# Second-layer scores as three 64-row products per head, two heads side by side in the array, and the PSUM banks split anew

## The chip, the core and the metric

The kernel runs on one core of one Trainium2 chip. The metric is device time in microseconds for one execution. TensorE (PE in the profile) multiplies, VectorE (DVE), ScalarE (ACT) and GpSimd (POOL) do the elementwise work, and SyncE (SP) issues the DMAs. PE writes its products into PSUM, of which a tile here is one bank (128 partitions by 512 fp32 numbers), and there are eight banks.

## What is computed

A trunk of two layers over 2048 tokens plus 16 learned meta tokens, model width 1024, in fp32. The first layer runs a sliding-window attention and a convolution branch side by side. The second layer is a stick-breaking attention with 16 heads of 64 dimensions: for every query the sigmoids of the scores are combined by a running product from the diagonal back to the first key.

```python
# second layer, per block of 128 queries (16 heads, d = 64)
z = einsum('bqhd,bkhd->bhqk', q_block, k[:, :kend]) * d ** -0.5
log_beta = log_sigmoid(z)
log_1m = where(valid, log_sigmoid(-z), 0.0)          # valid: key before query, not padding
after = cumsum(log_1m, axis=3, reverse=True) - log_1m
a = where(valid, exp(log_beta + after), 0.0)
out = einsum('bhqk,bkhd->bqhd', a, v[:, :kend])
# then: out * silu(gate) @ w_out, post-norm, residual
```

The products need more precision than one pass of the array's reduced fp32 format (fp32r) gives, so a matrix is split into a high and a low part, x = hi + lo, and a product is summed from hi·hi, hi·lo and lo·hi (and, in the scores before the change, lo·lo as well).

## The kernel before

Everything is written with a tile framework. The code emits steps, `interleave` mixes two lists of steps by weight (attention of one head pair with the projection of another), and a scheduler then sets the order of the instructions on each engine, with priorities that `tc.high_priority` raises. Each engine runs its instructions in that fixed order. An instruction that waits holds up all behind it on its engine.

The first layer (`layer0`) takes four token chunks: `stage1` projects (24 matmuls per unit of 128 output columns, `mm3` at lines 138 to 140), `stage2` does the window attention and the convolution branch, then `outp` the output projection. The second layer (`layer1`) goes over eight head pairs p and two halves of the queries hf (0: query blocks 0 to 7, 1: blocks 8 to 15). `proj(p, hf)` projects k, q, v and gate, unit by unit: 24 matmuls into one bank, then an evacuation. For k and q that is an ACT copy (line 777) and a DVE subtraction (line 778), for v an ACT copy (line 786), for the gate an ACT sigmoid (804) and a DVE multiply (805).

`attn(p, hf)` does the attention of two heads h. Queries come in pairs m of two 128-blocks x, keys in chunks of up to 512 columns, from the diagonal backwards. For each chunk:

- scores (line 907): per h and x one bank z and two matmuls of 128 rows. The stationary operand is q's high (i = 0) or low (i = 1) part, stored twice over in the 64+64 rows; the moving operand is `kst` of that head, with k's high part in rows 0 to 63 and its low part in rows 64 to 127.
- ACT reads the bank twice: `om` = sigmoid(−z) (line 914) and `be` = sigmoid(z) (line 915). The bank is free when `be` has been read.
- DVE runs the product scan `S` (line 920) and multiplies (line 921).
- PE transposes `be` by 128-column blocks into `pt` (line 939), ACT copies to `aT` (line 945), and PE adds up `av` (line 953), with the two heads in the two 64-column halves of the array, in one run per chunk at raised priority.

There are 192 such chunks (24 per head pair). Operands are loaded from DRAM by SP: `kst` once per pass, the q tiles `qt` for each m, in eight DMAs (line 883).

Eight banks are shared out as pools: `pj` 2 (projections), `pz` 3 (scores, and in the first layer also transposes and every second projection unit), `pt` 2 (transposes), `pav` 1 (`av`). In the first layer `banks = cycle(BK)` alternates `stage1`'s units between `pj` and `pz`; `pw` (line 541) and `po` (line 640), and in the second layer all projections (line 764) and the output projection (line 1004), use `pj` alone.

Of the kernel before, what the change touches and what calls it, by code (L numbers as in the profile page):

```python
# [34 lines left out]
CB = 6  # L35
PB = (2, 3, 2)
BK = ("pj", "pz")
WP = 60
AVP = 400
PRE0 = 1  # L40
PRE1 = 3
# [37 lines left out]
class Trunk:  # L79
# [108 lines left out]
    def layer0(self, after=None):  # L188
# [300 lines left out]
        def cbranch(ut):  # L489
# [44 lines left out]
            def pw():  # L534
                ch, cl = S["ch"], S["cl"]
                gb = w2.tile([P, 4, 272], F32, tag="gb", name="gb", bufs=1)
                nc.sync.dma_start(gb[:, :, :N], gbd[:, :, b0 : b0 + N].rearrange("r p t -> p r t"))
                for m in range(4):
                    if m % 2 == 0:
                        wh, wl = self.weights(pww, a["w_pw2"][m // 2], w2, "yl", f"wp{m // 2}")  # L540
                    ps = self.bank("pj", "pw")
                    for k in range(4):
                        kk = 4 * (m % 2) + k
                        self.mm3(ps[:, :N], wh[:, kk], wl[:, kk], ch[:, k, :N], cl[:, k, :N], k == 0, k == 3)
                    tt = w2.tile([P, 272], F32, tag="ctt", name="mc")
                    nc.vector.tensor_tensor(tt[:, :N], ps[:, :N], gb[:, m, :N], ALU.mult)
                    nc.sync.dma_start(md[4 + m, :, b0 : b0 + N], tt[:, :N])
# [78 lines left out]
        def outp(t):  # L626
# [3 lines left out]
            def mm(nh):  # L630
# [8 lines left out]
                w = slice(nh * 512, nh * 512 + 512)  # L639
                ps = self.bank("pj", "po")  # L640
                for k in range(KB):
# [91 lines left out]
    def after0(self, pool, tags):  # L733
        self.layer1_pools()
        self.evs = (pool, tags, D, 2)
        self.H, self.gates, self.tags = {}, [], cycle(("raw", "wh", "wl", "wh", "wl"))
        steps = self.load_part(0, 0) + self.load_part(0, 1)
# [8 lines left out]
        def proj(p, hf, parts=(0, 1)):  # L746
# [11 lines left out]
            def unit(m, part, c0, n, evac):  # L758
                def go():
                    th, tl, h0 = H[hf, part]  # L760
                    if m not in W:
                        W[m] = wload(m)
                    wh, wl = W[m]
                    ps = self.bank("pj", "pj1")
                    s = slice(c0 - h0, c0 - h0 + n)
                    with self.behind():
                        for k in range(KB):
                            self.mm3(ps[:, :n], wh[:, k], wl[:, k], th[:, k, s], tl[:, k, s], k == 0, k == KB - 1)
                    evac(ps[:, :n], c0, n)

                steps.append((float(n), go))
# [47 lines left out]
    def layer1(self):  # L819
# [12 lines left out]
        def attn(p, hf):  # L832
# [5 lines left out]
            def start():  # L838
                S["k"] = ks = []
                n = NM + nt * P  # L840
                for h in range(2):
                    kst = w4.tile([P, T], F32R, tag="kst", name="kst")
                    for i in range(2):
                        self.mv(kst[i * HD : i * HD + HD, :n], kd[i][p, h * HD : h * HD + HD, :n])
                    ks.append(kst)
# [30 lines left out]
            def qload(m):  # L876
                q0 = NM + m * 2 * P
                S["q"] = qs = []
                for h in range(2):
                    for i in range(2):  # L880
                        qt = w2.tile([P, 256], F32R, tag=f"q{h}{i}", name="qt")
                        for j in range(2):
                            self.mv(qt[j * HD : j * HD + HD], qd[i][p, h * HD : h * HD + HD, q0 : q0 + 256])
                        qs.append(qt)

            def pair_steps(m):
# [5 lines left out]
                def chunk(ei):  # L892
# [6 lines left out]
                    nbs = [b1 - b0 - (1 if first else 0), b1 - b0]  # L899
                    for h in range(2):  # L900
                        for x in range(2):
                            n = nbs[x] * P + mo
                            if n == 0:
                                continue
                            z = self.bank("pz", "z")
                            for i in range(2):
                                nc.tensor.matmul(z[:, :n], S["q"][2 * h + i][:, x * P : x * P + P], S["k"][h][:, k0 : k0 + n], start=(i == 0), stop=(i == 1))  # L907
                            om = w3.tile([P, 513], F32, tag="om", name="om")
# [5 lines left out]
                            nc.scalar.activation(om[:, :n], z[:, :n], AF.Sigmoid, scale=-0.125)  # L914
                            nc.scalar.activation(be[:, :n], z[:, :n], AF.Sigmoid, scale=0.125)  # L915
                            if first:
# [74 lines left out]
        def outp(t):  # L991
            S = {}

            def mm(nh):
# [8 lines left out]
                w = slice(nh * 512, nh * 512 + 512)  # L1003
                ps = self.bank("pj", "po1")
                for k in range(KB):
# [36 lines left out]
        for _, f in self.first + proj(1, 0):  # L1042
            f()
        for p in range(2, 6):
            interleave(proj(p, 0), attn(p - 2, 0))
# [83 lines left out]
```

## Time and profile before

| | us |
|---|---|
| median of 3 runs (2906.99 to 2913.82) | 2910.22 |
| the profiled execution's own time | 2916.46 |
| its span, first to last instruction | 2914.7 |
| first and last score matmul (line 907) start at | 1077.0 and 2821.9 |
| PE busy | 2742.9 (94%) |
| DVE busy | 2214.4 (76%) |
| ACT busy | 1463.5 (50%) |
| POOL busy | 775.3 (27%) |

Busy time of PE counts a matmul from its start to its modelled end, and matmuls overlap. What a matmul costs in a stream is the distance from its start to the start of the next one. A row of the timeline merges equal instructions that follow each other (x4 is four of them) and gives the start of the first. An entry such as `128*64 128x256` is a product in 128 rows and 64 columns of the array with 256 moving columns. An fp32 matmul of the program (`av`) is two rows of the trace, an fp32r one (scores, projections) is one.

### The profile page before, as it was taken

What the parts mean: (1) busy time and instruction counts of PE and PEld (TensorE: products, weight loads), DVE (VectorE), ACT (ScalarE), POOL (GpSimd) and SP (SyncE); (2) the same over time, 40 slices, a digit from 0 to 9 for tenths busy, and PEclk for the clock granted to TensorE, in tenths of its full rate; (3) what the DMA queues carried; (4) which work ended last, traced back from release to release, by engine and by line L of the source; (5) the groups of instructions that cost most, each with busy time, mean ns of one, the idle gap of its engine ahead of it and who ended that gap; (6) DMA issues with size and microseconds to landing.
All of it is one profiled execution on the core that took longest, in us unless ns stands there. A gap on an engine that the chain in (4) does not pass through costs nothing.

```text
span 2914.7 us, 49596 instructions
## 1 busy us (share of the span) xinstructions
PE 2742.9 (94%) x16110; PEld 2191.9 (75%) x16110; DVE 2214.4 (76%) x3696; ACT 1463.5 (50%) x3568; POOL 775.3 (27%) x2679
## 2 busy tenths in 40 slices
PE   7888989989899999999999899999999999999997
PEld 6877767767688898888887677777777777766876
DVE  7997878878767753666568888878888887887864
ACT  4223434332445432555545666767666766655551
POOL 4431211000000212333335632323223322333210
PEclk9899999999999999999999999999999999999999
DMA  7877779778866665444445562423232332244322
GB/s 264 279 247 224 235 242 266 232 229 249 264 188 206 216 189 155 132 135 133 121 136 175 148 168 69 120 68 109 66 103 82 94 110 73 74 129 125 113 94 90
DMA packets 303986, 462.87 MB, mean 159 GB/s; under 512 B 46640, under 2 KB 200640, under 8 KB 300656
## 3 DMA queue, kind: packets, MB, share of 16 engines
q1 hardware_dynamic: 303728, 459.70, 52.4%
q8 instruction: 129, 2.11, 0.3%
q14 instruction: 129, 1.06, 0.1%
HBM read 312.16 MB, written 142.14 MB: 156 GB/s over the span
## 4 chain that ended last, share of the span: by engine, by line
PE 68%; DVE 10%; DMA 9%; issue 5%; ACT 3%; POOL 2%; SPq 2%; DVEq 0%; ACTq 0%; POOLq 0%
PE pj L140 10%; PE pj L138 10%; PE pj L139 10%; PE z L907 7%; PE av L953 7%; PE pt L939 6%; PE po L138 4%; PE po L140 4%; PE po L139 4%; DVE y L304 3%; DMA wl<-wk 3%; DVE S L920 2%; DMA raw<-in_w_in 1%; DVE be L921 1%; DMA md<-mc 1%
## 5 line engine op out<-in xcount | busy, mean ns | idle before, releaser
L920 DVE TENSOR_TENSOR_SCAN S<-om,be 128x401 f32<-128x401 f32 (+3 forms) x512 | 536.3, 1068 | 72.4 <-ACT om L914 51.7
L914 ACT ACTIVATE om<-z 128x384 f32<-128x384 f32 (+5 forms) x768 | 377.7, 510 | 200.0 <-PE z L907 132.9
L921 DVE TENSOR_TENSOR be<-be,S 128x385 f32<-128x385 f32 (+5 forms) x768 | 413.8, 563 | 76.2 <-POOL be L912 21.8
L138 PE MATMUL pj<-th,wh 128*128 128x512 f32 (+2 forms) x1280 | 460.5, 360 | 6.9 <-DVE ev L805 3.6
L140 PE MATMUL pj<-th,wl 128*128 128x512 f32 (+2 forms) x1280 | 452.8, 354 | 0.0
L139 PE MATMUL pj<-tl,wh 128*128 128x512 f32 (+2 forms) x1280 | 450.6, 352 | 0.0
L945 ACT COPY aT<-pt 128x512 f32<-128x512 f32 (+2 forms) x672 | 333.9, 504 | 192.6 <-PE pt L939 152.9
L907 PE MATMUL z<-kst,qt 128*128 128x384 f32 (+6 forms) x1536 | 394.9, 357 | 31.3 <-ACT be L915 29.5
L915 ACT ACTIVATE be<-z 128x384 f32<-128x384 f32 (+5 forms) x768 | 375.2, 505 | 72.4 <-PE pt L939 71.7
L304 DVE SCALAR_TENSOR_TENSOR y<-u,cw,y 128x512 f32<-128x512 f32 (+1 forms) x480 | 392.1, 822 | 8.0
L939 PE MATMUL pt<-ident,be 128*128 128x128 f32 x2176 | 361.4, 280 | 17.8 <-ACT ev L794 6.2
L138 PE MATMUL pj<-hTh,wh 128*128 128x512 f32 (+2 forms) x880 | 322.9, 368 | 30.7 <-DMA wh<-wk 18.7
L140 PE MATMUL pj<-hTh,wl 128*128 128x512 f32 (+2 forms) x880 | 321.2, 367 | 30.4 <-POOL wl L128 15.4
L939 PEld LDWEIGHTS pt<-ident,be 128*128 128x128 f32 x2176 | 251.4, 141 | 113.9 <-ACT aT L945 31.4
L139 PE MATMUL pj<-hTl,wh 128*128 128x512 f32 (+2 forms) x880 | 318.5, 362 | 0.8 <-DVE hTl L186 0.8
L907 PEld LDWEIGHTS z<-kst,qt 128*128 128x128 f32 x1536 | 247.7, 190 | 76.1 <-ACT be L915 55.6
L953 PE MATMUL av<-aT,vt 128*64 128x256 f32 (+1 forms) x2304 | 281.9, 380 | 4.4 <-DVE og L971 4.3
L911 POOL MEMSET om<- 128x1 f32 x768 | 74.6, 99 | 768.9 <-DVE S L920 753.9
L138 PEld LDWEIGHTS pj<-th,wh 128*128 128x128 f32 x1280 | 241.6, 189 | 33.7 <-DVE ev L805 4.6
L140 PEld LDWEIGHTS pj<-th,wl 128*128 128x128 f32 x1280 | 240.9, 188 | 30.2 <-DVE wl L110 0.3
L139 PEld LDWEIGHTS pj<-tl,wh 128*128 128x128 f32 x1280 | 241.4, 189 | 25.1 <-issue 0.4
L920 DVE TENSOR_TENSOR_SCAN S<-om 128x257 f32<-128x257 f32 (+4 forms) x256 | 204.6, 811 | 62.8 <-POOL om L918 49.9
(177 smaller groups left out, 4482.5 us busy)
## 6 DMA issues: line engine op xcount, KB each, us to landing
raw<-in_w_in SPq DMA_DIRECT2D x98, 512.0 KB, 3.9
wh<-wk SPq DMA_DIRECT2D x66, 512.0 KB, 5.2
wl<-wk SPq DMA_DIRECT2D x66, 512.0 KB, 6.1
qt<-qhd SPq DMA_DIRECT2D x256, 64.0 KB, 2.6
qt<-qld SPq DMA_DIRECT2D x256, 64.0 KB, 2.4
wk<-wh SPq DMA_DIRECT2D x22, 512.0 KB, 5.1
wk<-wl SPq DMA_DIRECT2D x22, 512.0 KB, 4.6
kst<-khd SPq DMA_DIRECT2D x16, 516.0 KB, 7.4
```

The source lines that it names most:

```text
L138: mm(out, sh, mh, start=first, stop=False)
L139: mm(out, sh, ml, start=False, stop=False)
L140: mm(out, sl, mh, start=False, stop=last)
L304: return lambda: nc.vector.scalar_tensor_tensor(y[:, :TC], u[:, w : w + TC], cw[:, j, w : w + 1], y[:, :TC], ALU.mult, ALU.add)
L907: nc.tensor.matmul(z[:, :n], S["q"][2 * h + i][:, x * P : x * P + P], S["k"][h][:, k0 : k0 + n], start=(i == 0), stop=(i == 1))
L914: nc.scalar.activation(om[:, :n], z[:, :n], AF.Sigmoid, scale=-0.125)
L915: nc.scalar.activation(be[:, :n], z[:, :n], AF.Sigmoid, scale=0.125)
L920: nc.vector.tensor_tensor_scan(P_[:, : n + 1][:, ::-1], om[:, : n + 1][:, ::-1], om[:, : n + 1][:, ::-1], init, ALU.mult, ALU.bypass)
L921: nc.vector.tensor_tensor(bl[:, : n + 1], bl[:, : n + 1], P_[:, : n + 1], ALU.mult)
L939: nc.tensor.transpose(pt[:, o : o + P], bes[h, x][:, mo + b * P : mo + b * P + P], self.ident)
L945: cps.append(nc.scalar.copy(aT[:, lo:hi], pt[:, lo:hi]))
L953: mi = nc.tensor.matmul(av[h * HD : h * HD + HD, qc0 + x0 : qc0 + 256], S["v"][:, b0 + b, h * HD : h * HD + HD], at, start=not S["started" ...
```

## The change

1. The scores. Per head three products of 64 rows, hi·hi, hi·lo, lo·hi, replace the two of 128 rows. Head 0 lies in rows 0 to 63, head 1 in rows 64 to 127, so that the two heads' products use different halves of the array and write to different banks. A key chunk has 12 such products instead of 8. `kst` and `qt` now hold both heads, one tile for high and one for low, so a pair m loads its queries in two DMAs instead of eight (half the bytes), and k comes in two DMAs instead of four.
2. One run per key chunk. All four z tiles are taken first, the 12 products are emitted together at priority ZP = 800, and the first of them waits for the last four `be` (`zread[-4:]`), that is, until all four banks of the chunk before have been read.
3. Banks. PB goes from (2, 3, 2) to (1, 4, 2): one bank for `pj`, four for `pz`. In the first layer `pw` and `po` now alternate between the pools as `stage1` does. In the second layer units alternate before the attention starts and after it has ended; while it runs, projections and the output projection have the one bank of `pj`.

```diff
-PB = (2, 3, 2)
+PB = (1, 4, 2)
+ZP = 800
...
@@ pw and, in the same way, outp of the first layer
-                    ps = self.bank("pj", "pw")
+                    ps = self.bank(next(banks), "pw")
...
@@ proj and, in the same way, outp of the second layer
-                    ps = self.bank("pj", "pj1")
+                    ps = self.bank(next(self.free), "pj1")
...
@@ attn: start
-                for h in range(2):
+                for i in range(2):
                     kst = w4.tile([P, T], F32R, tag="kst", name="kst")
-                    for i in range(2):
-                        self.mv(kst[i * HD : i * HD + HD, :n], kd[i][p, h * HD : h * HD + HD, :n])
+                    self.mv(kst[:, :n], kd[i][p, :, :n])
...
@@ attn: qload
-                for h in range(2):
-                    for i in range(2):
-                        qt = w2.tile([P, 256], F32R, tag=f"q{h}{i}", name="qt")
-                        for j in range(2):
-                            self.mv(qt[j * HD : j * HD + HD], qd[i][p, h * HD : h * HD + HD, q0 : q0 + 256])
-                        qs.append(qt)
+                for i in range(2):
+                    qt = w2.tile([P, 256], F32R, tag=f"q{i}", name="qt")
+                    self.mv(qt, qd[i][p, :, q0 : q0 + 256])
+                    qs.append(qt)
...
@@ attn: chunk
-                    for h in range(2):
-                        for x in range(2):
+                    zs, wait = {}, self.zread[-4:]
+                    for x in range(2):
+                        n = nbs[x] * P + mo
+                        if n == 0:
+                            continue
+                        for h in range(2):
+                            zs[h, x] = self.bank("pz", "z")
+                        with tc.high_priority(offset=ZP):
+                            for i, j in ((0, 0), (0, 1), (1, 0)):
+                                for h in range(2):
+                                    r = slice(h * HD, h * HD + HD)
+                                    mi = nc.tensor.matmul(zs[h, x][:, :n], S["q"][i][r, x * P : x * P + P], S["k"][j][r, k0 : k0 + n], start=(i + j == 0), stop=(i == 1))
+                                    if wait is not None:
+                                        self.after_all(mi, wait)
+                                        wait = None
+                    for x in range(2):
+                        for h in range(2):
                             n = nbs[x] * P + mo
                             if n == 0:
                                 continue
-                            z = self.bank("pz", "z")
-                            for i in range(2):
-                                nc.tensor.matmul(z[:, :n], S["q"][2 * h + i][:, x * P : x * P + P], S["k"][h][:, k0 : k0 + n], start=(i == 0), stop=(i == 1))
+                            z = zs[h, x]
...
-                            nc.scalar.activation(be[:, :n], z[:, :n], AF.Sigmoid, scale=0.125)
+                            self.zread.append(nc.scalar.activation(be[:, :n], z[:, :n], AF.Sigmoid, scale=0.125))
...
@@ layer1
         for _, f in self.first + proj(1, 0):
             f()
+        self.free = cycle(("pj",))
...
+        self.free = cycle(BK)
         for t in range(8, NT):
```

(`self.free` and `self.zread` are set up in `after0`, with `self.free = cycle(BK)`.) Lines after the first additions move by 1 to 14: the scores are line 910 after the change, `mm3` lines 139 to 141, `om` and `be` 926 and 927, transposes 951, `aT` copies 957, `av` 965, the evacuations 779, 780, 788, 806 and 807.

What the scheduler makes of it is seen in three places of the instruction order. First the scores of a key chunk on PE, in the second half of the queries. Before (z is a score bank, pt a transpose, ptv a transpose of v):

```order
L907 MATMUL z<-kst,qt 128x256 x2
L907 MATMUL z<-kst,qt 128x384 x2
L953 MATMUL av_24083<-aT,vt_23339 64x256 x8
L939 MATMUL pt_24359<-ident,be 128x128 x4
L907 MATMUL z<-kst,qt 128x256 x2
L939 MATMUL pt_24366<-ident,be 128x128 x4
L939 MATMUL pt_24373<-ident,be 128x128 x4
L907 MATMUL z<-kst,qt 128x384 x2
L793 MATMUL ptv_24422<-ident,ev_24419 128x128
L907 MATMUL z<-kst,qt 128x384 x4
L953 MATMUL av_24083<-aT,vt_23339 64x256 x8
```

And now one chunk's run, with buffer numbers. The four banks are z_25038 (head 0, x 0), z_25039 (head 1, x 0), z_25046 (head 0, x 1) and z_25047 (head 1, x 1); the kst and qt named are the high or the low part:

```order
L910 MATMUL z_25038<-kst_23377,qt_24620 128x400
L910 MATMUL z_25039<-kst_23377,qt_24620 128x400
L910 MATMUL z_25046<-kst_23377,qt_24620 128x400
L910 MATMUL z_25047<-kst_23377,qt_24620 128x400
L910 MATMUL z_25038<-kst_23379,qt_24620 128x400
L910 MATMUL z_25046<-kst_23379,qt_24620 128x400
L910 MATMUL z_25039<-kst_23379,qt_24620 128x400
L910 MATMUL z_25047<-kst_23379,qt_24620 128x400
L910 MATMUL z_25038<-kst_23377,qt_24622 128x400
L910 MATMUL z_25046<-kst_23377,qt_24622 128x400
L910 MATMUL z_25047<-kst_23377,qt_24622 128x400
L910 MATMUL z_25039<-kst_23377,qt_24622 128x400
```

Before, the score products stood in twos and fours between other work. Now all 12 stand together, and the scheduler has put the heads in the order 0 1 0 1, 0 0 1 1, 0 0 1 1. Of the 194 runs in the program 190 have this order of heads.

Second, what lies between that run and the next on PE, and beside it on ACT. PE now:

```order
L910 MATMUL z<-kst,qt 128x400 x12
L951 MATMUL pt_24868<-ident,be 128x128 x2
L951 MATMUL pt_24873<-ident,be 128x128 x2
L951 MATMUL pt_24972<-ident,be 128x128 x4
L965 MATMUL av_24137<-aT,vt_23381 64x256 x6
L951 MATMUL pt_24979<-ident,be 128x128 x4
L910 MATMUL z<-kst,qt 128x256 x2
```

ACT now, in the same place:

```order
L926 ACTIVATE om<-z 128x400 x3
L927 ACTIVATE be<-z 128x400
L957 COPY aT<-pt_24868 128x256
L927 ACTIVATE be<-z 128x400 x2
L957 COPY aT<-pt_24873 128x256
L926 ACTIVATE om<-z 128x400
L927 ACTIVATE be<-z 128x400
```

Before, a z product waited for its own bank alone, the third back. Now the first of the next run stands behind all eight reads of ACT and the two copies among them, with 12 transposes and 6 `av` products of PE in between.

Third, two projection units that follow each other on PE, in the first half of the queries. Before:

```order
L139 MATMUL pj1_13935<-tl1_9540,wh1_13750 128x512
L140 MATMUL pj1_13935<-th1_9539,wl1_13751 128x512
L138 MATMUL pj1_13972<-th0_9537,wh1_13968 128x272
L139 MATMUL pj1_13972<-tl0_9538,wh1_13968 128x272
L140 MATMUL pj1_13972<-th0_9537,wl1_13969 128x272
```

Now:

```order
L140 MATMUL pj1_13921<-tl1_9540,wh1_13740 128x512
L141 MATMUL pj1_13921<-th1_9539,wl1_13741 128x512
L139 MATMUL pj1_13958<-th0_9537,wh1_13954 128x272
L140 MATMUL pj1_13958<-tl0_9538,wh1_13954 128x272
L141 MATMUL pj1_13958<-th0_9537,wl1_13955 128x272
```

The rows are alike, but before the second unit went into the other bank of `pj`; now it goes into the bank that the first has just filled.

More of the change, by code (lines that the diff above doesn't have):

```diff
@@ L639, in mm @@
                 w = slice(nh * 512, nh * 512 + 512)
-                ps = self.bank("pj", "po")
+                ps = self.bank(next(banks), "po")
                 for k in range(KB):
@@ L735, in after0 @@
         self.evs = (pool, tags, D, 2)
+        self.zread, self.free = [], cycle(BK)
         self.H, self.gates, self.tags = {}, [], cycle(("raw", "wh", "wl", "wh", "wl"))
@@ L1003, in mm @@
                 w = slice(nh * 512, nh * 512 + 512)
-                ps = self.bank("pj", "po1")
+                ps = self.bank(next(self.free), "po1")
                 for k in range(KB):
```

## Prediction

> **What bounds the kernel now.** I read the stretches of the span first, then the chain of waits, then the scores by shape and in order of time. In the stretches the columns are the stretch, its length, and the busy time of PE, its weight loads, DVE, ACT and POOL; the attention of the second layer runs from 1077 us, its second half of the queries from about 1600 us.
>
> ```profile
> 1077.00:1600.00 523.00, 514.57 (x3542) 445.98 (x3542) 318.41 (x501) 245.53 (x724) 195.71 (x706) 1.00 0.48 141
> 1600.00:2650.00 1050.00, 998.82 (x5976) 741.63 (x5976) 878.17 (x1154) 692.18 (x1691) 347.48 (x1526) 0.99 0.36 103
> ...
> PE 68%; DVE 10%; DMA 9%; issue 5%; ACT 3%; POOL 2%; SPq 2%; DVEq 0%; ACTq 0%; POOLq 0%
> ```
>
> PE is busy 98% and 95% of the two stretches, DVE 61% and 84%, ACT 47% and 66%, at a granted clock of 0.99 to 1.00; the chain that ended last is PE for 68% of the span. So in the changed part the time is the length of PE's instruction stream plus the stops in it. The halved q loads are worth nothing: the only wait of the scores for a transfer is the 0.2 us of the last row below.
>
> What PE waits for, four rows of its list (total us, times, longest; the second is of the first layer):
>
> ```profile
> PE z L907 <- ACT be L915: 29.5, 52, 2.1
> PE pj L138 <- DMA wh<-wk: 18.7, 9, 5.0
> PE pj L138 <- DVE ev L805: 3.6, 5, 0.7
> PE z L907 <- DMA kst<-kld: 0.2, 1, 0.2
> ```
>
> **The scores, by shape.** Five groups hold 1472 of the 1536 products:
>
> ```profile
> L907 PE MATMUL z<-kst,qt 128*128 128x384 f32 x512 | 138.3, 364 | 10.4 <-ACT be L915 9.5 <-DVE be L921 0.3
> L907 PE MATMUL z<-kst,qt 128*128 128x400 f32 x320 | 89.2, 372 | 10.2 <-ACT be L915 10.1
> L907 PE MATMUL z<-kst,qt 128*128 128x512 f32 x256 | 84.0, 421 | 5.8 <-ACT be L915 5.2
> L907 PE MATMUL z<-kst,qt 128*128 128x256 f32 x224 | 50.6, 307 | 1.4 <-ACT be L915 1.4
> L907 PE MATMUL z<-kst,qt 128*128 128x272 f32 x160 | 34.6, 312 | 3.3 <-ACT be L915 3.3
> ```
>
> Their mean durations overlap, so I take distances of starts, from places in the timeline where nothing waits (start, duration, instruction):
>
> ```profile
> 2012.13 0.52 PE L907 MATMUL z<-kst,qt 128*128 128x384 f32 x2
> 2012.49 0.39 PE L138 MATMUL pj<-th,wh 128*128 128x512 f32 x1
> ...
> 1168.57 1.25 PE L907 MATMUL z<-kst,qt 128*128 128x400 f32 x6
> 1169.66 0.28 PE L138 MATMUL pj<-th,wh 128*128 128x256 f32 x1
> ...
> 2217.95 0.62 PE L907 MATMUL z<-kst,qt 128*128 128x512 f32 x2
> 2218.41 0.40 PE L139 MATMUL pj<-tl,wh 128*128 128x512 f32 x1
> ...
> 2026.82 0.40 PE L907 MATMUL z<-kst,qt 128*128 128x256 f32 x2
> 2027.06 0.39 PE L138 MATMUL pj<-th,wh 128*128 128x512 f32 x1
> ```
>
> That is 0.36/2 = 0.18 us for 384 columns, 1.09/6 = 0.18 for 400, 0.46/2 = 0.23 for 512 and 0.24/2 = 0.12 for 256. With 0.12 for all the narrower ones, the scores take 832 × 0.18 + 256 × 0.23 + 448 × 0.12 = 262 us of PE's stream.
>
> **Term 1, the products: −33 us.** No 64-row pair is in this trace; the nearest are `av`'s products, in two 64-column halves. The second pair of rows is full-array fp32 products, for scale:
>
> ```profile
> 1700.06 0.54 PE L907 MATMUL z<-kst,qt 128*128 128x272 f32 x3
> 1700.53 1.52 PE L953 MATMUL av<-aT,vt 128*64 128x256 f32 x12
> 1701.97 0.66 PE L939 MATMUL pt<-ident,be 128*128 128x128 f32 x4
> 1702.39 0.48 PE L138 MATMUL pj<-th,wh 128*128 128x512 f32 x1
> ...
> 2647.18 1.05 PE L969 MATMUL av<-amT,zvm 128*128 128x128 f32 x8
> 2648.06 0.60 PE L939 MATMUL pt<-ident,be 128*128 128x128 f32 x4
> ```
>
> A full-array row takes 0.88/8 = 0.11 us for 128 columns, so 0.22 for 256; twelve would take 2.64 us. `av`'s twelve take 1.44: two halves do run side by side, at 0.22 per pair (six are 1.3 us) plus some overhead. I take the same of row halves. If heads alternated, 12 products would fill 6 places where there were 8, −25% or −66 us. But the order of the heads in a run is 0 1 0 1 0 0 1 1 0 0 1 1, and PE starts its products in the order of the program: the fifth product (head 0) has the sixth (head 0) behind it and runs alone, the pairs shift by one, and the twelfth runs alone too. That is 7 places: −1/8 of 262 = −33 us. Bounds: −66 (six places) and +131 (no halves side by side, 12 places).
>
> **Term 2, dividing the array: +65 us.** The `av` run also shows what a change of division costs. Before it three 272-column scores (0.12 to 0.13 each) take 0.47 instead of 0.38: +0.09. The run takes 1.44 instead of 1.30: +0.14, of which the first pair's exposed weight load is a part. Behind it four transposes take 0.42. Without a change before them they take 0.35, and the same is seen of a row-divided product (a 16-row transpose among 128-row ones):
>
> ```profile
> 349.48 0.39 PE L140 MATMUL pj<-hTh,wl 128*128 128x512 f32 x1
> 349.80 0.60 PE L525 MATMUL pt_c<-ident,yn 16*128 16x16 f32 x3
> 350.15 0.47 PE L138 MATMUL pj<-hTh,wh 128*128 128x512 f32 x1
> ...
> 2223.23 0.60 PE L939 MATMUL pt<-ident,be 128*128 128x128 f32 x4
> 2223.58 0.98 PE L907 MATMUL z<-kst,qt 128*128 128x400 f32 x4
> ```
>
> There and back is 0.09 + 0.14 + 0.07 = 0.30 us for columns. For rows it is 0.32 − 0.23 = 0.09 going in, and the three transposes take 0.35, as long as four, 0.10 more: 0.19, the lower bound, since its one product has 16 columns and hides nothing. A score run's first pair loads 128 weight columns instead of 64, half of 0.11 more, so I take 0.34 (upper bound 0.36). In the program's order the array's division changes 446 times before and 825 times after (a score run next to an `av` run costs one change, not two): 379 more, 190 there-and-backs, 65 us (36 to 68).
>
> The Trainium skill, "TensorEngine Tiling (Array Packing)", Key Properties, says that changing the tiling mode drains TensorE while different tiles of one mode work in parallel; the trace agrees on the first (0.09 us before either kind of division), and shows the second for columns only. By its "up to 2×" for 64-row products this change would be −66 us in term 1, were it not for the order of the heads.
>
> **Term 3, one bank of `pj`: +27 us.** Evacuations (mean ns behind the comma):
>
> ```profile
> L777 ACT CAST ev<-pj 128x512 fp32r<-128x512 f32 x48 | 28.2, 587 | 71.0 <-PE pj L140 67.5 <-issue 3.4
> L778 DVE TENSOR_TENSOR ev<-pj,ev 128x512 fp32r<-128x512 f32 x48 | 33.0, 689 | 48.7 <-ACT ev L777 48.7
> L786 ACT COPY ev<-pj 128x512 f32<-128x512 f32 x24 | 14.1, 589 | 26.6 <-PE pj L140 26.6
> L804 ACT ACTIVATE ev<-pj 128x512 f32<-128x512 f32 x24 | 14.8, 615 | 17.7 <-PE pj L140 17.7
> L805 DVE TENSOR_TENSOR ev<-pj,ev 128x512 f32<-128x512 f32 x24 | 16.5, 686 | 25.2 <-ACT ev L804 25.2
> ```
>
> A unit now waits until the one before has left the bank: 1.28 us for k and q (587 + 689), 0.59 for v, 1.30 for the gate, and some 0.15 of hand-over. Between neighbouring units in the new order I counted PE's other work, at 0.11 per transpose. Behind k and q units seven gaps hold nothing (short by 1.43 each, 10 us) and five hold two transposes (1.21 each, 6 us); behind v units seven hold two (0.52 each, 4 us); the rest, gates and output units among them, are short by 7 us together. The cover for all other units is the attention of the chunk, over 2 us. The sum, 27, has no idle work to fall back on, as PE runs in order; the lower bound is 15 (if only the empty gaps and those of two transposes behind k and q count), the upper 45 (ACT found busy with a sigmoid each time, 0.5 more at 36 of these places).
>
> **Term 4, all four banks at once: +20 us.** The first product of a run now holds up PE until ACT has read four banks:
>
> ```profile
> L915 ACT ACTIVATE be<-z 128x400 f32<-128x400 f32 x160 | 81.5, 529 | 17.6 <-PE pt L939 17.5
> L914 ACT ACTIVATE om<-z 128x400 f32<-128x400 f32 x160 | 81.4, 529 | 34.0 <-PE z L907 19.7 <-DVE S L920 7.9 <-issue 3.7
> L945 ACT COPY aT<-pt 128x256 f32<-128x256 f32 x160 | 62.2, 389 | 10.5 <-PE pt L939 9.9
> ```
>
> At the place shown in the order, ACT has 8 × 0.53 + 2 × 0.39 = 5.0 us to do, and can begin two places (0.36 us) before the run's end, when the first bank is complete. PE has 12 transposes (1.3), 6 `av` (1.3) and the changes of division (0.5): 3.1 us. It stands 1.5 us or longer, and transposes, `av` and the next DVE chain stand behind it. The same count over all runs is short at 42 of 189 places, by 56 us. Against it goes the wait that was there, 29.5. I take +20 rather than +27, as stops of term 3 give ACT time; bounds 0 and +40.
>
> **Everything else: 0.** In the first layer units alternate between the pools as before and a unit of 24 products covers the evacuation of the other pool's; DVE's work is unchanged, and with PE longer its 84% falls. The output projection behind the attention alternates over more banks, where PE has no stop to lose.
>
> **Sum.** −33 + 65 + 27 + 20 = +79. The profiled execution's own time was 2916.5, 6 above the median of the runs, so 2910 + 79 = 2989; I say 2990.
>
> **Rivals.** (a) *Halves fill six places*, because each row half takes its own products without regard to the other's: term 1 is −66, the time 2957; if the narrower loads also let a pair run nearer to its column rate, another −20, 2937. For it: `av`'s pairs lose less per product than full-array ones. Against it: nothing in the trace starts out of order. (b) *Weight loads bind the pairs*: two 128-column loads of 0.11 us each per pair, one after the other, make a pair 0.22 where a 400-column score takes 0.18. A run is then 12 × 0.11 plus the last product, about 1.5 to 1.7 us instead of 1.44 for 384 columns, some +43 over the kernel instead of −33: 3066. (c) *Row halves of fp32r do not run side by side*: +131 instead of −33: 3154. "TensorE: Matmul & The Clock Gate" of the Trainium skill, Part 3, gives row tiles starting about 4 ns apart, which speaks against (c); no run so far shows it. (d) *Faster*: the new banks of the first layer reorder its 1077 us, where PE's stops come to
>
> ```profile
> 0.00:1077.00 1077.00, 981.36 (x5308) 806.91 (x5309) 845.05 (x1748) 416.53 (x918) 183.24 (x283) 0.97 0.77 236
> ```
>
> 1077 − 981 = 96 us. `pw` and `po` in other banks would have to win back over 79 of them; at 96 it gives 2893. Against it: the largest of those stops is a transfer (the 18.7 us above), no bank.
>
> **Chances.** My forecast 0.64, own range 2950 to 3030 (terms 2 to 4 at their bounds, not all together); (a) 0.14, (b) 0.09, (c) 0.05, (d) 0.08. The likeliest is 2990. The range takes in (a) and (b): 2930 to 3080. A difference of 0.2% (6 us) is about what a measurement here can tell from none. Faster 0.08, which is (d), the same 0.04 from the low end of (a), slower 0.88.
>
> **What would show it.** 2304 score products; in a run of 400 columns starts 7 places apart, 1.3 us, with fifth and twelfth alone (term 1). About 0.09 before a run and 0.1 behind it (term 2). Waits of PE for `ev` at L807 and L780 of some 27 us (term 3), and for `be` of 45 to 60 us (term 4). DVE and ACT busy time as before. I am wrong if a run takes six places or twelve, or if the scores' wait falls below 29.5 because the scheduler's gaps are filled by late work.

## The result, and the profile after

| kernel | us, median | ratio to before, 95% interval |
|---|---|---|
| before, in the same comparison | 2908.82 | 1 |
| changed | 3064.11 (3056.87 to 3066.31) | 1.0523 [1.0506, 1.0539] |

Slower by 5.2%, 155 us; 2990 was forecast, with a range up to 3080. The profiled execution has a span of 3055.2 us. The stretches of the attention, with the columns of before (stretch, length, then busy PE, weight loads, DVE, ACT, POOL, granted clock), and the line of the chain:

```profile
1077.00:1600.00 523.00, 492.73 (x3473) 403.30 (x3471) 300.14 (x480) 234.39 (x693) 173.86 (x688) 0.99 0.36 113
1600.00:2650.00 1050.00, 913.86 (x5903) 655.61 (x5903) 778.93 (x1038) 622.66 (x1525) 320.97 (x1384) 0.97 0.25 84
```

```profile
PE 68%; DVE 9%; ACT 9%; DMA 7%; issue 5%; POOL 2%; SPq 1%; DVEq 0%; ACTq 0%; POOLq 0%
```

PE is busy 94% and 87% of the two stretches where it was 98% and 95%, and ACT's share of the chain goes from 3% to 9%. No other engine has become the bound: DVE and ACT have 2197.9 and 1459.8 us of work, no more than before. PE simply stops more, and its list of waits says for what (total us, times, longest):

```profile
PE pt L951 <- ACT aT L957: 72.9, 72, 3.9
PE av L965 <- ACT aT L957: 49.2, 72, 3.6
PE pj L139 <- DVE ev L780: 17.1, 10, 2.7
PE pj L139 <- DMA wh<-wk: 14.3, 8, 3.8
PE pt L951 <- ACT ev L796: 13.7, 16, 2.7
...
PE z L910 <- ACT be L927: 1.2, 2, 1.0
```

The scores themselves hardly wait any more (29.5 us before, 1.2 now), though the new wait was put on them. What PE waits for is ACT's copies of transposed tiles: as whole lists, 6.0 us before in one row, and 72.9 and 49.2 now in the two largest.

Between the first score product and the last lie 1745.1 us before and 1855.2 after, so 110 of the 140 us between the two profiled executions arise there. PE's idle time in it, added up over its instructions, goes from 61.2 to 194.9: +134. The rest, PE's stream without its stops, became 24 us shorter. Two things are in that number. Projections left the stretch: 289 products of the second layer's projections now run ahead of it and 71 of the output projection behind it, by the distances of their starts 45 and 16 us. And the stops are paid a second time, in the granted clock (the share of full speed that PE is given). One place in the changed kernel, as three stretches of 3.4 us (with the columns above), and some of PE's products there:

```profile
1305.00:1308.40 3.40, 1.25 (x8) 0.93 (x8) 3.28 (x6) 1.49 (x5) 1.29 (x8) 1.00 0.34 101
1308.40:1311.80 3.40, 3.40 (x9) 2.63 (x8) 0.59 (x2) 0.00 (x0) 0.00 (x0) 0.50 0.11 39
1311.80:1315.20 3.40, 3.40 (x18) 2.31 (x18) 0.00 (x0) 0.00 (x0) 0.00 (x0) 1.00 0.00 0
```

```profile
1307.84 0.50 PE L139 MATMUL pj<-th,wh 128*128 128x512 f32 x1 [2.15 <-DVE ev L780]
...
1309.27 0.63 PE L140 MATMUL pj<-tl,wh 128*128 128x512 f32 x1
1309.70 0.63 PE L141 MATMUL pj<-th,wl 128*128 128x512 f32 x1
```

PE waits 2.15 us, then the clock is at half for 3.4 us, and products of 512 columns start 0.43 us apart instead of the 0.23 at full clock. Between the first and the last score product there are 4 stretches at half clock before the change and 24 after it (20 and 116 us). Each of the 24 comes directly behind 3.4 us in which PE stood idle for 37% or more of the time. With 0.43 for 0.23, an estimate of what the half clock costs is 8 us before and 46 after: +38. The 61 us that left and these 38 make −23 of the −24.

The same sum over the whole execution: of the 140 us, idle time makes 115 (163.0 and 278.2) and the half clock by this estimate 25 (43 and 68). Nothing is left for the three 64-row products and all changes of the array's division together. For other kernels below the sum does not come out as closely, so it is good to some 25 us.

How the stops look. First PE in a stretch without projections before the change (start, duration, instruction, idle time before it):

```profile
1709.25 0.50 PE L907 MATMUL z<-kst,qt 128*128 128x256 f32 x2 [0.34 <-ACT be L915]
1709.80 0.66 PE L939 MATMUL pt<-ident,be 128*128 128x128 f32 x4
1710.21 0.59 PE L907 MATMUL z<-kst,qt 128*128 128x384 f32 x2
1710.73 1.30 PE L953 MATMUL av<-aT,vt 128*64 128x256 f32 x12
1711.96 0.66 PE L939 MATMUL pt<-ident,be 128*128 128x128 f32 x4
1712.38 0.49 PE L907 MATMUL z<-kst,qt 128*128 128x256 f32 x2
1712.70 0.38 PE L939 MATMUL pt<-ident,be 128*128 128x128 f32 x2
```

Two score products stand behind each group of transposes, and while they run ACT copies. The same kind of stretch after the change, PE first and then ACT:

```profile
2028.89 1.36 PE L910 MATMUL z<-kst,qt 64*128 64x400 f32 x12
2030.19 0.66 PE L951 MATMUL pt<-ident,be 128*128 128x128 f32 x4
2032.17 0.66 PE L951 MATMUL pt<-ident,be 128*128 128x128 f32 x4 [1.32 <-ACT aT L957]
2033.24 1.52 PE L965 MATMUL av<-aT,vt 128*64 128x256 f32 x12 [0.41 <-ACT aT L957]
...
2039.13 0.66 PE L951 MATMUL pt<-ident,be 128*128 128x128 f32 x4 [1.69 <-ACT aT L957]
2040.81 1.95 PE L965 MATMUL av<-aT,vt 128*64 128x256 f32 x16 [1.02 <-ACT aT L957]
```

```profile
2030.16 1.29 ACT L926 ACTIVATE om<-z 128x400 f32<-128x400 f32 x3 [0.57 <-PE z L910]
2031.33 0.53 ACT L927 ACTIVATE be<-z 128x400 f32<-128x400 f32 x1
2031.71 0.40 ACT L957 COPY aT<-pt 128x256 f32<-128x256 f32 x1
2031.96 0.96 ACT L927 ACTIVATE be<-z 128x400 f32<-128x400 f32 x2
2032.74 0.44 ACT L957 COPY aT<-pt 128x256 f32<-128x256 f32 x1
```

Twelve score products run at once, and ACT, idle for 0.57 us until then, gets four banks to read. The copy that PE's next transposes need (2031.71) stands behind three `om` and one `be`, PE stops for 1.32 us, and it has no score products left to put there. ACT waits more for scores too, though it has the same work:

```profile
ACT om L926 <- PE z L910: 261.5, 159, 8.9
```

against 132.9 us before (`om` on line 914 for `z`). Both engines wait for each other in turn.

### The profile page after: what moved, and what is told of

Same layout as the page of the kernel before. It is cut to its first block, busy times and chain, and to the rows that moved or that the text cites. A ratio compares the mean times of both kernels' runs of the same rounds, so it can differ in the third digit from the quotient of the medians.

```text
span 3055.2 us, 49925 instructions
## 1 busy us (share of the span) xinstructions
PE 2768.2 (91%) x16878; PEld 2153.5 (70%) x16878; DVE 2197.9 (72%) x3696; ACT 1459.8 (48%) x3566; POOL 767.7 (25%) x2679
## 4 chain that ended last, share of the span: by engine, by line
PE 68%; DVE 9%; ACT 9%; DMA 7%; issue 5%; POOL 2%; SPq 1%; DVEq 0%; ACTq 0%; POOLq 0%
PE pj L139 11%; PE pj L141 11%; PE pj L140 10%; PE av L965 8%; PE z L910 6%; PE pt L951 6%; PE po L139 3%; PE po L140 3%; PE po L141 3%; ACT be L927 2%; DVE y L305 2%; ACT om L926 2%; DMA wl<-wk 2%; DVE S L932 2%; ACT aT L957 2%
## 5 line engine op out<-in xcount | busy, mean ns | idle before, releaser
L932 DVE TENSOR_TENSOR_SCAN S<-om,be 128x401 f32<-128x401 f32 (+3 forms) x512 | 527.6, 1068 | 241.7 <-ACT om L926 216.3
L926 ACT ACTIVATE om<-z 128x384 f32<-128x384 f32 (+5 forms) x768 | 343.7, 490 | 379.6 <-PE z L910 261.5
L139 PE MATMUL pj<-th,wh 128*128 128x512 f32 (+2 forms) x1280 | 467.2, 365 | 30.1 <-DVE ev L780 17.1
L140 PE MATMUL pj<-tl,wh 128*128 128x512 f32 (+2 forms) x1280 | 456.8, 357 | 0.0
L951 PE MATMUL pt<-ident,be 128*128 128x128 f32 x2176 | 357.5, 287 | 91.4 <-ACT aT L957 72.9
L927 ACT ACTIVATE be<-z 128x384 f32<-128x384 f32 (+5 forms) x768 | 384.0, 518 | 35.9 <-PE pt L951 35.8
L305 DVE SCALAR_TENSOR_TENSOR y<-u,cw,y 128x512 f32<-128x512 f32 (+1 forms) x480 | 385.2, 814 | 5.7
L965 PE MATMUL av<-aT,vt 128*64 128x256 f32 (+1 forms) x2304 | 314.4, 395 | 50.3 <-ACT aT L957 49.2
L965 PEld LDWEIGHTS av<-aT,vt 128*64 128x64 f32 x2304 | 159.9, 142 | 162.9 <-ACT aT L957 73.0
L932 DVE TENSOR_TENSOR_SCAN S<-om 128x385 f32<-128x385 f32 (+4 forms) x256 | 199.6, 800 | 95.9 <-POOL om L930 42.1
L910 PE MATMUL z<-kst,qt 64*128 64x384 f32 (+6 forms) x2304 | 248.8, 347 | 1.2 <-ACT be L927 1.2
```

The costliest lines, as they stand in the source:

```text
L139: mm(out, sh, mh, start=first, stop=False)
L140: mm(out, sh, ml, start=False, stop=False)
L305: return lambda: nc.vector.scalar_tensor_tensor(y[:, :TC], u[:, w : w + TC], cw[:, j, w : w + 1], y[:, :TC], ALU.mult, ALU.add)
L910: mi = nc.tensor.matmul(zs[h, x][:, :n], S["q"][i][r, x * P : x * P + P], S["k"][j][r, k0 : k0 + n], start=(i + j == 0), stop=(i == 1))
L927: self.zread.append(nc.scalar.activation(be[:, :n], z[:, :n], AF.Sigmoid, scale=0.125))
L932: nc.vector.tensor_tensor_scan(P_[:, : n + 1][:, ::-1], om[:, : n + 1][:, ::-1], om[:, : n + 1][:, ::-1], init, ALU.mult, ALU.bypass)
```

## The experiments

The theories as the expectations name them. Theory 1: four banks at once, that is the run of a chunk and its wait for all four banks. Theory 2: the single bank of the projections. Theory 3: dividing the array by rows. "Idle" below is PE's idle time between the first and last score product, and "changes" are those of the array's division in the same stretch, both added up over the rows of the trace: 61.2 us and 378 before, 194.9 and 755 after.

**The run without row division.** 128-row products as before (with the q and k tiles and loads that they need), in runs of eight, with the waits, banks and priority of the changed kernel:

```diff
-  for i, j in ((0, 0), (0, 1), (1, 0)):
+  for i in range(2):
     for h in range(2):
-      mi = nc.tensor.matmul(zs[h, x][:, :n], S["q"][i][r, ...], S["k"][j][r, k0 : k0 + n], ...)
+      mi = nc.tensor.matmul(zs[h, x][:, :n], S["q"][2 * h + i][:, ...], S["k"][h][:, k0 : k0 + n], ...)
```

> The changed kernel with the score products of before (two of 128 rows per head, no row halves) still in one run per key chunk, with the wait for all four banks and the new bank split. Theory 1 (the loss comes from taking four banks at once: PE's next run waits for eight sigmoids, and ACT's copies of the transposes stand behind them): waits stay as in the changed kernel, products are 262 us instead of about 196, changes of division 488 instead of 825 (some 57 us less), so 3064 + 66 - 57 = about 3070 (3040 to 3090). Theory 2 (one bank for the projections makes the loss): the same, about 3070. Theory 3 (dividing the array by rows makes the loss): about 2910 + 50, at most 2970.

Measured 3048.95 us, 1.0479 [1.0462, 1.0495]. PE's first two waits:

```profile
PE pt L953 <- ACT aT L959: 63.8, 73, 3.3
PE av L967 <- ACT aT L959: 51.0, 74, 1.6
```

Nearly the whole loss, and the same waits, without one row-divided product. Theory 3 falls as the main cause: the division adds 15 us.

**The banks alone.** The kernel before with PB = (1, 4, 2) and the units alternating as in the change:

```diff
-PB = (2, 3, 2)
+PB = (1, 4, 2)
...
-  ps = self.bank("pj", "pj1")
+  ps = self.bank(next(self.free), "pj1")
```

> The kernel before with nothing changed but the banks: PB (1, 4, 2) and the units' alternation as in the changed kernel; scores as before, each waiting for its own bank. Theory 1: only the wait for the one projection bank comes in (about 20 us in the trace of the changed kernel), and a fourth score bank takes some of the 29.5 us away: 2905 to 2935. Theory 2: most of the loss is here, 3000 or more. Theory 3: no change, 2910.

Measured 2937.4 us, 1.0096 [1.0079, 1.0114]: 28 us, 2 above Theory 1's numbers and far from Theory 2's 3000, so Theory 2 falls as the main cause, and a fourth bank for scores wins nothing back (they wait 40.8 us for `be`, 29.5 before).

**Two runs of six, each waiting for its own two banks.**

```diff
-  zs, wait = {}, self.zread[-4:]
+  zs, prev = {}, self.zread[-4:]
...
+  wait = prev[2 * x : 2 * x + 2]
```

> The changed kernel with two runs of six products per key chunk, one per query block, each waiting only for the two banks it writes. The array's division changes 1048 times instead of 825, 223 x 0.17 = 38 us more. Theory 1: PE's waits in the attention (195 us in the changed kernel's trace) fall by 70 to 100, so 3064 - 85 + 38 = 3015 (2990 to 3040). Theories 2 and 3: waits as they are, 3100.

Measured 3064.79 us, 1.0524 [1.0497, 1.0551], as the changed kernel, and between the numbers of Theory 1 and those of 2 and 3. Two effects cancel: idle falls from 194.9 to 159.8, −35 us, and the changes rise from 755 to 979, 112 there-and-backs, which at 0.34 us are +38.

**One ACT read per bank.** `be` is worked out on GpSimd as 1 − `om`:

```diff
-  nc.scalar.activation(om[:, :n], z[:, :n], AF.Sigmoid, scale=-0.125)
-  self.zread.append(nc.scalar.activation(be[:, :n], z[:, :n], AF.Sigmoid, scale=0.125))
+  self.zread.append(nc.scalar.activation(om[:, :n], z[:, :n], AF.Sigmoid, scale=-0.125))
+  nc.gpsimd.tensor_scalar(be[:, :n], om[:, :n], -1.0, 1.0, ALU.mult, ALU.add)
```

> The changed kernel with each score bank read once: be is taken as 1 - om on GpSimd instead of a second sigmoid on ScalarE, so ACT has four reads per chunk instead of eight. Theory 1: the bank wait and the queue in front of the copies halve, 3064 - (60 to 110) = 2955 to 3005, unless GpSimd becomes late itself. Theories 2 and 3: no change but a few us, 3050 to 3075.

Measured 3068.24 us, 1.0551 [1.0530, 1.0572]. Theory 1's numbers are missed; those of 2 and 3 fit, which the two runs above ruled out as the main cause. Its groups:

```profile
L927 POOL TENSOR_SCALAR be<-om 128x384 f32<-128x384 f32 (+5 forms) x768 | 585.4, 764 | 28.3 <-ACT om L926 27.8
...
L926 ACT ACTIVATE om<-z 128x384 f32<-128x384 f32 (+5 forms) x768 | 343.7, 479 | 622.0 <-DVE S L932 369.5 <-PE z L910 164.8 <-POOL be L927 33.0
```

ACT's busy time falls from 1459.8 to 1199.0 us, but ACT now waits 369.5 us for scans, that is for one of the three buffers of `om`. The run does not tell how the reads alone count. It raised a new theory, A: the batch of four tiles is stopped by the three buffers of `om`, and the copies stand behind the stopped ACT. Its rivals were B, the raised priority of the run, and C, the wait for all four banks.

**Five buffers for `om`.** In the changed kernel: `om = w3.tile([P, 513], F32, tag="om", name="om", bufs=5)`.

> The changed kernel with five buffers instead of three for om, the first sigmoid of a score tile; nothing else. Theory A (a run fills four score tiles at once but om has three buffers: ScalarE stops at the fourth om until VectorE has scanned the first, and the copies of transposed tiles that TensorE waits for stand behind it): 2960 to 3020 us, ScalarE's waits for scans (om <- S, 61.5 us in the changed kernel) under 15, TensorE's waits for aT (132 us in the attention stage) under 70. Theory B (the run is put too early in the queues by its raised priority) and theory C (the wait for all four banks itself makes ScalarE idle before the run and overfull after it): 3050 to 3075, waits for aT above 110.

Measured 3066.04 us, 1.0529 [1.0503, 1.0555]. ACT's wait for scans, 61.5 us in the changed kernel, is gone; PE's two rows of waits for `aT` are 112 us instead of 122, and the time has not moved:

```profile
ACT om L926 <- DVE S L932: 1.7, 2, 1.5
```

Theory A falls. The same buffers in the kernel with two runs:

> The kernel with two runs of six products, each waiting for its own two banks (3065 us), with five buffers for om instead of three. Theory A (om buffers): 2980 to 3035 us, ScalarE's waits for scans from 40.5 to under 10. Theories B and C: 3050 to 3075.

Measured 3040.81 us, 1.0440 [1.0416, 1.0464]: 24 us less than with three buffers, inside neither A's nor B's and C's numbers. Idle falls by 12 us. The other half goes with the clock: the mean granted clock is 0.973 to 0.978 in the four executions with three buffers and 0.978 to 0.982 in the four with five, and the two traces have 23 and 13 stretches at half clock among their scores.

**The changed kernel without the priority** (ZP = 0):

> The changed kernel without the raised priority of the score run (ZP 0 instead of 800): the run then stands where the program writes it, most runs still of six pairs or of three. Theory B (too early by its priority): 2960 to 3010 us. Theories A (three om buffers) and C (the wait for all four banks): 3045 to 3085, since both leave the batch of four tiles as it is.

Measured 3042.90 us, 1.0448 [1.0418, 1.0478]: 21 us better, just below what A and C expected and far from B's 3010.

**128-row products without the wait for all four:**

```diff
-  zs, wait = {}, self.zread[-4:]
+  zs, wait = {}, None
```

> The kernel with 128-row products in runs of eight (3049 us) without the wait for all four banks: each score tile's two products go as soon as their own bank is free, in the same program order (both heads and both query blocks ahead of the transposes), with the same raised priority and the same banks (1, 4, 2). Theory C (the wait for all four): 2920 to 2960 us. Theory B (priority): 3020 to 3055. Theory A (om buffers): 2930 to 2990, since the fourth om still stops ScalarE but TensorE has its other products to go on with.

Measured 2984.40 us, 1.0245 [1.0224, 1.0266]: 65 us of the loss were the wait. It is more than B allows and less than C claimed; A's numbers would fit, but A fell by the run above.

```profile
PE pt L953 <- ACT aT L959: 34.8, 58, 1.8
PE pj L139 <- DVE ev L780: 19.5, 18, 2.9
PE z L912 <- ACT be L929: 17.1, 36, 1.8
```

The stop moves back to where the forecast had looked for it: transposes wait 34.8 instead of 63.8, the `av` run has left the list's head, and scores wait 17.1 for `be`. PE's order has changed with it: the wait held the eight products of a chunk together (190 groups of eight in the trace of the run without row division), and without it they stand in 507 twos and 126 fours. So the 65 us are the wait together with the collecting that it brings; no run has one without the other.

**The same without the priority:**

> The kernel with 128-row products and no wait for all four banks (2984 us) without the raised priority as well: left of the change are the banks (1, 4, 2) and the order of the program, in which a chunk's four score tiles stand ahead of its transposes, query block by query block. Theory B2 (the rest of the loss, 47 us against the kernel with the banks alone, is the priority): 2930 to 2955 us. Theory D (it is the program order, four tiles ahead): 2970 to 2995.

Measured 2945.99 us, 1.0112 [1.0084, 1.0140], as B2 says: 38 us are the priority. What the program order adds to the banks alone (2937) lies within the intervals. The priority's 38 are less well placed than the wait: 8 are idle time (100.9 to 109.0), 14 are changes of division (378 to 460, as scores now cut into `av` runs), and the rest I cannot assign.

**With the wait and without the priority:**

> The kernel with 128-row products and the wait for all four banks (3049 us) without the raised priority: the fourth corner of a square whose others are neither (2946 us), priority alone (2984) and both (3049). If wait and priority add up (65 and 38): 3011 us, 3000 to 3020. If they share a cause, and the priority costs only the 21 us that it cost in the changed kernel: 3022 to 3038. In both cases the wait alone makes the larger part of the loss, 55 us or more above 2946.

Measured 2998.56 us, 1.0309 [1.0289, 1.0330], 1 us below the range for adding up and far from the other; of the 55 us that either asked of the wait alone it shows 53. The square for 128-row products, with the row-divided kernel beside it:

| | no priority | priority |
|---|---|---|
| no wait for all four | 2946 | 2984 |
| wait for all four | 2999 | 3049 |
| wait, three 64-row products | 3043 | 3064 |

Wait alone is 53 us, priority alone 38, both together 103, 12 more than their sum. PE waits for `aT` in the attention for 23.6, 36.2, 107.2 and 125.6 us in the four corners (no wait; priority; wait; both).

**Row halves and the order of the program.** The changed kernel with the head in the outer loop:

```diff
-  for i, j in ((0, 0), (0, 1), (1, 0)):
-    for h in range(2):
+  for h in range(2):
+    for i, j in ((0, 0), (0, 1), (1, 0)):
```

> The changed kernel with the products of a query block written head by head (0 0 0 1 1 1 0 0 0 1 1 1) instead of 0101 0011 0011 with the head in the inner loop; same waits, banks and priority. If each half of the array takes its own products whenever it is free: a run of twelve still fills six places (400 columns: about 1.02 us from the first start to the last), head 1's first product starts within some 10 ns of head 0's first, and the time is that of the changed kernel, 3050 to 3080 us. If the halves start strictly in the order of the program, only neighbours of different heads overlap: nine places, 0.5 us more per run of twelve at 400 columns, 3120 to 3170 us.

Measured 3121.05 us, 1.0719 [1.0688, 1.0751]. A run of 400 columns with the same neighbours, in the changed kernel and then in this one:

```profile
1982.84 0.39 PE L140 MATMUL pj<-tl,wh 128*128 128x512 f32 x1
1983.16 1.37 PE L910 MATMUL z<-kst,qt 64*128 64x400 f32 x12
1984.46 1.09 PE L951 MATMUL pt<-ident,be 128*128 128x128 f32 x8
```

```profile
2022.44 0.39 PE L140 MATMUL pj<-tl,wh 128*128 128x512 f32 x1
2022.76 1.65 PE L910 MATMUL z<-kst,qt 64*128 64x400 f32 x12
2024.34 1.10 PE L951 MATMUL pt<-ident,be 128*128 128x128 f32 x8
```

From the run's start to the next transposes 1.30 and 1.58 us. The scheduler turned the written order into 0001 0001 1111 (head of each product) in PE's queue. The median starts in a run of 400 columns, in ns, as the trace has them and, for the second run, sorted into two rows by the 0.18 us that a half needs per product:

```
0101 0011 0011   0 3   287 290   470 473   650 655   833 838   1014 1019
0001 0001 1111   0     288       470       650       833       1014
                 10              476       765   946       1124      1307
```

In the changed kernel all twelve go in six pairs, 3 to 5 ns apart, although its queue has two of a head next to each other. In this run head 1's first product starts 10 ns after head 0's first, ahead of two products of head 0 that stand before it in the queue, and its second starts ahead of three. Then it falls behind, and its last two run alone: 0.29 us more per run, for 190 runs about 55 us, which is the measured difference (57). The time lies at the low end of the in-order range and the starts say otherwise: a half takes its products ahead of the other's, over two or three of them here, but not over any number.

**The best row-divided form** found: two runs of six, five `om` buffers, no priority.

> The kernel with two runs of six products, each waiting for its own two banks, and five om buffers (3041 us) without the raised priority. If the shares add up (priority 21 us in the changed kernel): 3010 to 3030 us. If the priority matters only where a run waits for all four banks: 3030 to 3055. In either case the time stays above 2937 us, the kernel with the banks alone, since two runs of six gain one place of about 0.17 us per run and pay 0.34 us for changing the array there and back.

Measured 3012.65 us, 1.0343 [1.0314, 1.0373]: the shares add up (28 us for the priority), and it stays above the banks alone. No form tried here beats the kernel before.

## Why the prediction was right, and where it was not

The time lay in the range and the sign was right, but the likeliest value was 74 us too low and the forecast's own range, 2950 to 3030, too low as well. Only the wider range holds the 3064. It reaches so far to take in rival (b), which happens to give 3066 but is not what took place: nothing binds the pairs. That is luck. The prediction also named two signs of being wrong, six places in a run and a scores' wait below 29.5 us, and both came. The steps:

**Term 1 (−33): wrong step, inside its bounds.** "PE starts its products in the order of the program", so fifth and twelfth alone: they are not. Rival (a)'s six places are what the starts show, so this term is −66 (two places in eight of 262 us). The prediction said it would be wrong in that case.

**Term 2 (+65): confirmed.** Going in costs 0.09 (0.32 instead of 0.23 ahead of the run above). In the run the first pair takes 0.287 instead of 0.18 (+0.11), and behind its last start come 0.27 instead of 0.18 (+0.09); the first transpose then takes 0.166 instead of 0.109 (+0.06). That is 0.34 or 0.35 there and back. With 755 changes for 378 the term is 188 × 0.34 = 64. The sum of terms 1 and 2 is then −2, and the balance of the two profiles above leaves about nothing, good to some 25 us. One experiment agrees, one less well: the two runs of six above balance to 3 us, but from the kernel with wait and without priority (378 changes) to the one with 64-row products (949) the sum is 286 × 0.34 − 66 = +31 with idle equal (161.0 and 162.5), and the measured difference is 44, of which the half clock makes 6 by the estimate above.

Against rival (c) stood "TensorE: Matmul & The Clock Gate" of the Trainium skill, Part 3, where row tiles start about 4 ns apart; the trace agrees, with 3 to 5 ns.

"TensorEngine Tiling (Array Packing)" of the Trainium skill, Key Properties, has both halves of this: different tiles of one mode work in parallel, and changing the mode drains the engine. The trace agrees with both, with pairs 3 to 5 ns apart and 0.34 us for a change there and back; it adds that with runs of twelve they cancel.

**Term 3 (+27): met in the net, by luck.** The banks alone cost +28, but in their profile two larger effects stand against each other. The first layer's last output product starts at 1013.1 us instead of 1037.9, a gain that the prediction put at nothing ("Everything else: 0"). Behind it the rest takes 41 us longer (the two executions are 16 us apart, the medians 28). Among the scores idle time goes from 61.2 to 97.8 us, and little of it is the wait that the term counted:

```profile
PE z L908 <- ACT be L916: 40.8, 53, 3.8
PE pt L940 <- ACT aT L946: 22.5, 31, 2.9
...
PE pj L138 <- DVE ev L779: 9.5, 10, 1.2
...
PE pj L138 <- DVE ev L806: 5.6, 7, 4.3
```

The last two rows are the projections' wait for their one bank, 15.1 us (3.6 before); scores and transposes wait 28 us more. In the changed kernel the waits for `ev` at L780 are 17.1 us and at L807 0.9.

**Term 4 (+20): the step that failed.** It counted how long the run would stand at its first product until ACT has read four banks, forecast 45 to 60 us of waits for `be`, and bounded the whole at +40. The wait for all four is worth 53 us without the raised priority and 65 with it, and PE stands elsewhere: 1.2 us for `be`, 122 us for `aT` in the two rows above. The count took the scores' own wait for the cost of the wait. By the two timelines and the run without the wait, where `aT` costs 36.2 us instead of 125.6, the cost is that score products no longer lie between transposes, where they gave ACT time to copy. The prediction's words for this case ("if the scores' wait falls below 29.5 because the scheduler's gaps are filled by late work") named the symptom, without a price for it.

**A term that was missing: the priority, +38.** "Everything else: 0" did not price ZP = 800. In the changed kernel itself it costs 21 us, with 128-row products 38 or 50.

The ladder by experiments, from 2909: banks +28, program order +9 (within the uncertainty), priority +38, wait for all four +65, rows +15, together 3064. The rows' 15 are 168 more there-and-backs (419 changes to 755), +57, less 66, and 15 more of idle time: +6. The 9 that remain are of the size by which executions of one kernel differ (3056.87 to 3066.31): the two profiled executions are 8 us apart, as is idle time over the whole of them (269.7 and 278.2). The 7 us that stay open in term 2's last comparison are the part of the row division that no run accounts for.

Rival (c), halves that don't run side by side, fell. (d) was right in kind and too small: in the changed kernel's profile too the first layer's last output product starts 24 us earlier (1013.6 for 1037.9; 1010 to 1023 in the other profiles with the new banks). PE's idle time ahead of the attention fell from 84.6 to 71.8 us, and its time at half clock there from 75 to 44. (d) needed over 79. There is one profile of the kernel before, and its execution is 8 us above the median of 2908.82.

## What to carry to other kernels

Where a chain of PE, ACT and DVE goes round per tile, small pieces of PE work between the steps are what hides the chain; collecting them into one run for the array's sake takes the cover away, and the stop appears at another instruction than the one that got the wait. Price a wait by what was interleaved before, not by the waiting instruction, and price a stop with the slower clock that follows it. Dividing the array by rows gains a quarter of the products' places and costs 0.34 us for each change there and back, so with 400 columns a run must save two places (0.36 us, twelve products for eight) to break even.

## What the runs showed of the hardware

- Two row halves of the array were not held to the order of the queue: with 0001 0001 1111 head 1's first two products started 10 and 476 ns into the run, ahead of two and three products of head 0 that the program has before them.
- Half clock followed stops much shorter than the stretch that it lasted. In the changed kernel's attention it came in stretches of 3.4 us (15 times), 6.8 (8) and 10.2 (1), each behind 3.4 us in which PE was idle for 37% or more, by short stops too: in half of the 24 cases the longest stop was 1.4 us or less. Products of 512 columns then started 427 ns apart (median) instead of 231.
- So the mean granted clock falls with the stops: 0.968 to 0.973 in the four executions of the changed kernel, 0.979 to 0.986 in those of the kernel before that the runs were compared with. The median distance of products, 231 ns in both, does not show it, because most products run at full clock.
